# A two-layer transformer block on one core: TensorE's order in the attention loop fixed by order edges

## The chip, the core and the metric

The kernel runs on one NeuronCore of a Trainium2 chip. Five engines work side by side and meet through semaphores: TensorE (PE, matmuls, its weight loads shown as PEld), VectorE (DVE), ScalarE (ACT), GpSimd (POOL) and SyncE (SP, which here issues most of the transfers). Matmul results go to PSUM, eight banks that are read by DVE and ACT. The metric is the device time of one execution in microseconds (us), the median of the runs.

## The reference

Two layers act on 256 tokens of width 2048 and on a context of 256 tokens. Layer 0 mixes by a Fourier transform and layer 1 by attention; each ends in a projection with `w_out`. The part that matters here is layer 1:

```python
def _attend_with_sink(q, k, v, sink, mask=None):
    s = jnp.einsum('bqhgd,bkhd->bhgqk', q, k) * (ATTN_HEAD_DIM ** -0.5)
    if mask is not None:
        s = jnp.where(mask, s, NEG_INF)
    sk = jnp.broadcast_to(sink[None, :, :, None, None], s.shape[:-1] + (1,))
    p = jax.nn.softmax(jnp.concatenate([s, sk], axis=-1), axis=-1)[..., :-1]
    return jnp.einsum('bhgqk,bkhd->bqhgd', p, v)
...
    q, k, v, z = jnp.split(h @ w_in, [D_BRANCH, D_BRANCH + kvw, D_BRANCH + 2 * kvw], axis=-1)
    ...
    y = o.reshape(b, n, D_BRANCH) * jax.nn.silu(z)
x = x + gate * (y @ w_out[1])
return _rmsnorm(x, final_g)
```

There are 64 query heads of width 64 in 8 groups, each group with one key and value head. A query sees 512 keys: 256 tokens (within a window) and 256 of the context. All is float32, which the kernel reaches by splitting each operand into a high and a low half and doing three matmuls for one.

## The kernel before, in words

The program is recorded by a layer (Tile) that orders each engine's instructions by a timeline of its own, in which the order of the code is the priority, and then puts in every semaphore wait. An engine works through its list in order. `tc.issue_after(ins)` adds an edge without a wait: each instruction that the block records on the engine of `ins` stands behind `ins` in that engine's list.

The attention loop treats the 64 heads as 32 pairs. For a pair `b` there are these steps:

- **Scores** (`stage_s`, L1504): for two token blocks and two heads, 12 matmuls of 512 columns into four PSUM banks. DVE adds the mask and takes the maximum of each (L1507), ACT takes the exponentials (L1511) and that of the sink (L1513), DVE makes the factor (`sm`, L1514 and L1515). Then the weights are scaled and split: the high half on ACT (L1526), the low half on DVE (L1527, both into `f`), and SP issues a transposing transfer of each of the four `f` into `ft` (L1529). For the last pair PE transposes instead (`pe_turn`, L1397).
- **Value product** (`stage_o`, L1538): 24 small matmuls of `ft` with the values into one bank; DVE then multiplies by the gate (`emit_y`, L1487).
- **Filler units** (`emit_unit`): the projections that are still to be done, cut into 142 units: 8 for each of eight q groups, 2 for each of 32 gates z, and 14 of the first quarter of the output projection. A unit is 12 matmuls of 512 columns (q and output, L145 to L147 of `mm3`) or 24 of 256 (z). Its weights come in as `raw` (three buffers, one for two units), ACT casts the high half `wh` and DVE subtracts the low half `wl` (L66 and L67 of `split`). `wh` and `wl` share six tiles, so three units can be ready.

When a q group is done (`finish_q`), ACT copies its two PSUM banks (L1369 and L1370), POOL applies the rotary embedding (L1132 to L1138), DVE makes a scale in four tiny operations on `sq` (L1376 to L1379), and the queries are split (`fq`, L1387 on ACT, L1388 on DVE) and transposed into `qt`; the first group is transposed by PE (L1397), copied out by ACT and DVE (L1398), the others by a transfer. A group serves four pairs, and each lap of four pairs is called a head below, after its key head. The output units need `y` split into `ys` (L66, low halves on POOL). Ten units go ahead of the loop; each lap then records scores, two units, the value product of the pair before, two units, and the scheduler may shift all of these on PE against each other.

Of the kernel before, what the change touches and what calls it, by code (L numbers as in the profile page):

```python
# [17 lines left out]
P = 128  # L18
D = 2048
KT = D // P  # L20
DB = 4096
NB = DB // P
# [10 lines left out]
def tile_dit(ctx: ExitStack, tc: tile.TileContext, a: dict, out: bass.AP):  # L33
# [1106 lines left out]
    with tc.tile_pool(name="h1", reuse_waits="tile", bufs=16) as h1p:  # L1140
# [130 lines left out]
        with tc.tile_pool(name="at", reuse_waits="tile", bufs=2) as at:  # L1271
# [55 lines left out]
            def o1_step(k, os_, wh, wl):  # L1327
                while len(yh) <= min(k + 4, NB - 1) and (len(yh) < 28 or fin):
                    y_split(len(yh))
                for tb in range(2):  # L1330
                    mm3(os_[tb], yh[k][:, tb * P : (tb + 1) * P], yh[k][:, N + tb * P : N + (tb + 1) * P], wh, wl, k == 0, k == NB - 1)
            slot = [0]

            def k_turn(hp):
# [95 lines left out]
                return half_split(raws1[src], i % 2)  # L1430

            ready = {}

            def emit_unit():
                if pos[0] >= len(ulist):
                    return
                u = ulist[pos[0]]
                if pos[0] not in ready:
                    ready[pos[0]] = prep(u)
                if pos[0] + 1 < len(ulist):  # L1440
                    ready[pos[0] + 1] = prep(ulist[pos[0] + 1])
                w = ready.pop(pos[0])
                pos[0] += 1
                kind, n, i, o = u
                if kind == "o":
                    if n == 0:
                        oA.extend([psum(), psum()])
                    for j in range(2):
                        o1_step(n * 2 + j, oA, *(t[:, j * 512 : (j + 1) * 512] for t in w))
                    return  # L1450
                wh, wl = w
                if kind == "q":
                    if i == 0:
                        o += [psum(), psum()]
                    if (n, i) == (0, 4):
                        with tc.issue_after(last_cast[0]):
                            prep_kk(0)
                    for j in range(2):
                        k = i * 2 + j
                        q = slice(j * 512, (j + 1) * 512)  # L1460
                        for tb in range(2):
                            mm3(o[tb], hx1[k][:, tb * P : (tb + 1) * P], hx1[k][:, N + tb * P : N + (tb + 1) * P], wh[:, q], wl[:, q], k == 0, k == KT - 1)
                    if i == 7:
                        finish_q(n, o)
                else:
                    if i == 0:
                        o.append(psum())
                    for k in range(i * 8, i * 8 + 8):
                        q = slice((k % 8) * P, (k % 8 + 1) * P)
                        mm3(o[0][:, 0:N], wh[:, q], wl[:, q], hx1[k][:, 0:N], hx1[k][:, N : 2 * N], k == 0, k == KT - 1)  # L1470
# [20 lines left out]
            def stage_s(b):  # L1491
# [6 lines left out]
                for tb in range(2):  # L1498
                    for hh in range(2):
                        so[hh, tb] = psum()  # L1500
                    for n, (jj, kx_) in enumerate(((j, kkh), (4 + j, kkh), (j, kkl))):
                        for hh in range(2):
                            r = slice(hh * 64, hh * 64 + 64)
                            PE.matmul(so[hh, tb], qt[r, jj, tb, :], kx_[r, :], start=n == 0, stop=n == 2)  # L1504
                    for hh in range(2):
                        o = so[hh, tb]
                        V.tensor_tensor_reduce(o, o, mask[:, tb, :], sc[:, tb : tb + 1], nsink[:, 2 * b + hh : 2 * b + hh + 1], ALU.add, ALU.min, mx[:, hh, tb : tb + 1])  # L1507
# [24 lines left out]
            def stage_o(blk, pair):  # L1532
# [2 lines left out]
                steps = [(kb, c, j) for kb in range(4) for c, j in ((0, kb), (64, kb), (0, 4 + kb))]  # L1535
                for n, (kb, c, j) in enumerate(steps):
                    for hh, ft in enumerate(pair):
                        PE.matmul(oo[hh * 64 : hh * 64 + 64, :], v01[kb][:, hk, c : c + 64], ft[:, j, :, :].rearrange("p t q -> p (t q)"), start=n == 0, stop=n == len(steps) - 1)  # L1538
                obs[blk, 1] = oo
                emit_y(blk)  # L1540

# [9 lines left out]
            while defer:  # L1551
                defer.pop(0)[1]()

            def filler():
                j = slot[0]
                slot[0] += 1
                emit_unit()
                if defer and defer[0][0] + 2 < j:
                    defer.pop(0)[1]()

            pts = {}
            for b in range(33):
# [16 lines left out]
                filler()  # L1579


        with tc.tile_pool(name="fin", reuse_waits="tile", bufs=1) as fp:
# [243 lines left out]
```

## Time and profile before

| | |
|---|---|
| median of 3 runs | 1780.81 us (1779.39 to 1782.48) |
| profiled execution, time | 1778.66 us |
| its span | 1776.9 us |
| mean granted clock of PE | 0.994 |
| PE busy | 1717.7 us (97%) |
| DVE busy | 1385.8 us (78%) |
| ACT busy | 1112.8 us (63%) |
| POOL busy | 342.2 us (19%) |
| attention loop, first scores to last value product | from 1132.4 to 1636.5 us |

The profile shows one execution. Times in its rows are microseconds from the span's start. Matmuls overlap in the pipeline, so a row's duration (0.38) is longer than the distance to the next start (0.233 for 512 columns), and a busy PE is not one at its peak: the pace is read from starts. In rows of the waits, the engine behind the arrow is the one whose work came last. In rows of stretches there stand start and end, length, busy time of PE, PEld, DVE, ACT and POOL with the number of instructions, PE's granted clock, the DMA engines' busy share and GB/s. Rows of the timeline hold start, duration, engine, line, operation, tiles, shape, count and, in brackets, the idle time ahead of it and what ended it. In rows of groups stand, behind the bar, busy time and mean ns of one, then the idle time ahead of them and its releasers.

### The profile page before, as it was taken

To read this page: it belongs to the slowest core of one execution; us is meant where nothing else is said; L and a number is where in the kernel's file an instruction comes from. 1 tells how busy PE (TensorE), PEld (TensorE's weight loads), DVE (VectorE), ACT (ScalarE), POOL (GpSimd) and SP (SyncE) were. 2 spreads that over 40 slices of the span, in tenths; PEclk is the share of its full clock that TensorE was granted. 3 is DMA by queue.
4 is the path that set the end of the run, shared out by engine and by line. 5 is a ranking of instruction groups with operands and counts; after the bars stand their busy time and mean duration, and the time that the engine had idled before them with its cause. 6 is when DMAs were issued, how large, how long until landed. Compare 5 with 4: busy or idle time off the path is not lost. (4 is left out here: it accounts for less than half of the span.)

```text
span 1776.9 us, 28302 instructions
## 1 busy us (share of the span) xinstructions
PE 1717.7 (97%) x10379; PEld 1134.2 (64%) x10379; DVE 1385.8 (78%) x2334; ACT 1112.8 (63%) x2125; POOL 342.2 (19%) x485
## 2 busy tenths in 40 slices
PE   6999999999999999999999999699999999999998
PEld 4679999544444444446445646588777777877464
DVE  5779888797777796877687786878888889887755
ACT  5545556477768745465235696666677777786643
POOL 0002111212222115112311122202202220251001
PEclk9999999999999999999999999899999999999999
DMA  9998998778998969976997692588798788888643
GB/s 394 417 354 254 277 274 244 301 286 315 327 308 313 318 224 368 357 285 261 378 339 222 213 351 104 166 199 197 211 243 207 201 223 231 201 209 289 222 177 119
DMA packets 249196, 469.95 MB, mean 264 GB/s; under 512 B 171392, under 2 KB 171792, under 8 KB 222176
## 3 DMA queue, kind: packets, MB, share of 16 engines
q1 hardware_dynamic: 197568, 335.60, 57.9%
q0 software_dynamic: 47344, 125.58, 22.2%
q10 hardware_dynamic: 4144, 6.95, 1.1%
q8 instruction: 81, 1.33, 0.3%
q14 instruction: 59, 0.48, 0.1%
HBM read 419.30 MB, written 12.59 MB: 243 GB/s over the span
## 5 line engine op out<-in xcount | busy, mean ns | idle before, releaser
L67 DVE TENSOR_TENSOR wl<-raw,wh 128x1024 fp32r<-128x1024 f32 x152 | 191.5, 1270 | 101.8 <-ACT wh L66 85.8
L66 ACT CAST wh<-raw 128x1024 fp32r<-128x1024 f32 x152 | 158.1, 1046 | 81.7 <-PE ps L146 61.8
L146 PE MATMUL ps<-act,wf 128*128 128x512 f16 x512 | 194.0, 379 | 0.0
L147 PE MATMUL ps<-act,wf 128*128 128x512 f16 x512 | 191.1, 379 | 0.0
L145 PE MATMUL ps<-act,wf 128*128 128x512 f16 x512 | 189.8, 379 | 0.6 <-ACT wf L137 0.2
L145 PE MATMUL ps<-y,wf 128*128 128x512 f16 x448 | 169.8, 379 | 0.8 <-ACT wf L137 0.8
L146 PE MATMUL ps<-y,wf 128*128 128x512 f16 x448 | 169.8, 379 | 0.0
L147 PEld LDWEIGHTS <-wf 128*128 128x128 f16 x960 | 93.9, 98 | 113.1
L145 PEld LDWEIGHTS <-wf 128*128 128x128 f16 x960 | 93.7, 98 | 113.2 <-ACT wf L137 4.2
L147 PE MATMUL ps<-y,wf 128*128 128x512 f16 x448 | 164.9, 379 | 0.0
L146 PEld LDWEIGHTS <-wf 128*128 128x128 f16 x960 | 93.9, 98 | 109.1
L147 PE MATMUL ps<-h,wl 128*128 128x256 f32 x512 | 144.6, 282 | 6.3 <-DVE wl L67 6.2
L145 PE MATMUL ps<-h,wh 128*128 128x256 f32 x512 | 147.4, 288 | 0.0
L137 ACT ACTIVATE wf<-raw,nrm 128x1024 f16<-128x1024 f32 x56 | 63.5, 1146 | 131.9 <-PE ps L147 71.2
L1511 ACT ACTIVATE p<-ps,mx 128x512 f32<-128x512 f32 x128 | 87.8, 687 | 89.1 <-DVE mx L1507 84.9
L146 PE MATMUL ps<-h,wh 128*128 128x256 f32 x512 | 143.6, 280 | 0.0
L138 DVE SCALAR_TENSOR_TENSOR wf<-raw,tn,wf 128x1024 f16<-128x1024 f32 x64 | 79.8, 1282 | 42.7 <-ACT wf L137 42.6
L829 ACT ACTIVATE act<-act 128x512 f32<-128x512 f32 x178 | 109.5, 617 | 5.0 <-DMA act<-in_wo 4.5
L790 POOL DMA_DIRECT2D wa<-in_adw x64 | 34.2, 535 | 370.6 <-PE ps L147 143.1
L1527 DVE SCALAR_TENSOR_TENSOR f<-p,sm,f 128x512 f16<-128x512 f32 x128 | 104.5, 870 | 1.4 <-ACT f L1526 1.4
L145 PEld LDWEIGHTS ps<-h,wh 128*128 128x128 f32 x512 | 96.8, 189 | 10.0 <-ACT th L1474 4.2
L145 PE MATMUL ps<-wh,h 128*128 128x512 f32 x256 | 102.8, 407 | 0.0
(436 smaller groups left out, 4799.8 us busy)
## 6 DMA issues: line engine op xcount, KB each, us to landing
raw<-in_wz SPq DMA_DIRECT2D x64, 1024.0 KB, 5.3
raw<-in_awp SPq DMA_DIRECT2D x32, 1024.0 KB, 12.7
zr<-in_adw SPq DMA_DIRECT2D x64, 512.0 KB, 6.9
wa<-in_adw POOLq DMA_DIRECT2D x64, 512.0 KB, 6.6
act<-in_wo POOLq DMA_DIRECT2D x128, 256.0 KB, 7.2
raw<-in_wo SPq DMA_DIRECT2D x32, 1024.0 KB, 8.4
raw<-in_wq SPq DMA_DIRECT2D x32, 1024.0 KB, 5.4
raw<-in_wu SPq DMA_DIRECT2D x32, 1016.0 KB, 7.0
```

What stands on the lines that cost most here:

```text
L66: last_cast[0] = S.copy(h, src).ins
L67: last_sub[0] = eng.tensor_tensor(l, src, h.bitcast(F32), op=ALU.subtract).ins
L137: last_cast[0] = S.activation(w[:, 0], src, AF.Copy, scale=up).ins
L138: last_sub[0] = V.scalar_tensor_tensor(w[:, 1], src, up, w[:, 0], op0=ALU.mult, op1=ALU.subtract).ins
L145: PE.matmul(o, wh, xh, start=start, stop=False)
L146: PE.matmul(o, wh, xl, start=False, stop=False)
L147: return PE.matmul(o, wl, xh, start=False, stop=stop).ins
L790: nc.gpsimd.dma_start(wf, a["adw"][i, kh, fg][:, q])
L829: S.activation(t, t, AF.Square, accum_out=c)
L1511: S.activation(pt[hh, tb], so[hh, tb], AF.Exp, bias=mx[:, hh, tb : tb + 1], scale=-1.0, accum_out=sm[:, hh, tb : tb + 1])
L1527: f_last[:] = fa, V.scalar_tensor_tensor(f[:, 512:1024], pt[hh, tb], s1, f[:, 0:512], op0=ALU.mult, op1=ALU.subtract).ins
```

## The change

The last matmul that was recorded is kept in `pe_last[0]`: the unit's (`mm3` and `o1_step` return theirs), the scores' or the value product's. Each unit, each `stage_s` and each block of `pe_turn` and `stage_o` is recorded within `tc.issue_after(pe_last[0])`, so all of its PE instructions stand behind the last matmul of the block recorded before it. And the loop's order is another: a pair's scores, four units, the value product of the pair before, the next pair's scores. In the last lap there are three units, then the transposes and the value product, then one unit. The edges bear on PE alone; DVE, ACT, POOL and SP are ordered anew by the scheduler's timeline.

```diff
@@ o1_step
                 for tb in range(2):
-                    mm3(os_[tb], yh[k][:, tb * P : (tb + 1) * P], ...)
+                    r = mm3(os_[tb], yh[k][:, tb * P : (tb + 1) * P], ...)
+                return r
@@ emit_unit
+            pe_last = [None]
...
-                        o1_step(n * 2 + j, oA, *(t[:, j * 512 : (j + 1) * 512] for t in w))
+                        pe_last[0] = o1_step(n * 2 + j, oA, *(t[:, j * 512 : (j + 1) * 512] for t in w))
...
-                            mm3(o[tb], hx1[k][:, tb * P : (tb + 1) * P], ...)
+                            pe_last[0] = mm3(o[tb], hx1[k][:, tb * P : (tb + 1) * P], ...)
...
-                        mm3(o[0][:, 0:N], wh[:, q], wl[:, q], ...)
+                        pe_last[0] = mm3(o[0][:, 0:N], wh[:, q], wl[:, q], ...)
@@ stage_s
-                            PE.matmul(so[hh, tb], qt[r, jj, tb, :], kx_[r, :], start=n == 0, stop=n == 2)
+                            pe_last[0] = PE.matmul(so[hh, tb], qt[r, jj, tb, :], kx_[r, :], start=n == 0, stop=n == 2).ins
@@ stage_o
-                        PE.matmul(oo[hh * 64 : hh * 64 + 64, :], ...)
+                        pe_last[0] = PE.matmul(oo[hh * 64 : hh * 64 + 64, :], ...).ins
@@ the loop
-            def filler():
-                j = slot[0]
-                slot[0] += 1
-                emit_unit()
-                if defer and defer[0][0] + 2 < j:
-                    defer.pop(0)[1]()
+            def filler(n):
+                for _ in range(n):
+                    j = slot[0]
+                    slot[0] += 1
+                    with tc.issue_after(pe_last[0]):
+                        emit_unit()
+                    if defer and defer[0][0] + 2 < j:
+                        defer.pop(0)[1]()
...
                 if b < 32:
-                    pts[b] = stage_s(b)
-                filler()
-                filler()
+                    with tc.issue_after(pe_last[0]):
+                        pts[b] = stage_s(b)
+                filler(4 if b < 32 else 3)
                 if b:
                     ft, fs = pts.pop(b - 1)
-                    for (hh, tb), f in fs.items():
-                        pe_turn(ft[hh], f, tb)
-                    stage_o(b - 1, ft)
-                filler()
-                filler()
+                    with tc.issue_after(pe_last[0]):
+                        for (hh, tb), f in fs.items():
+                            pe_turn(ft[hh], f, tb)
+                        stage_o(b - 1, ft)
+                if b == 32:
+                    filler(1)
```

PE's list before, where the second pair's scores end (L1504 scores, L1538 value product, L145 to L147 units):

```order
L1504 LDWEIGHTS qt
L1504 MATMUL ps<-kkl,qt 128x512
L1538 LDWEIGHTS v
L1538 MATMUL ps<-ft,v 64x256
L145 MATMUL ps<-h_10256,wh 128x256
L146 MATMUL ps<-h_10256,wh 128x256
L147 MATMUL ps<-h_10256,wl 128x256
```

There the first matmul of pair 0's value product stands behind pair 1's scores and ahead of the unit. PE's list now, at the first matmul of that product (L1540 now):

```order
L145 MATMUL ps<-h_10659,wh 128x256
L146 MATMUL ps<-h_10659,wh 128x256
L147 MATMUL ps<-h_10659,wl 128x256
L1540 LDWEIGHTS v
L1540 MATMUL ps<-ft,v 64x256
```

It has moved behind four whole units that follow pair 1's scores. DVE's list before, from the scale of the first q group to the first scores (wl are low halves of units, ISA ps,mx a mask and its maximum):

```order
L1379 TENSOR_SCALAR sq<-sq,ksc 128x2
L67 TENSOR_TENSOR wl<-raw,wh 128x1024
L1388 SCALAR_TENSOR_TENSOR fq<-act,sq,fq 128x512 x2
L67 TENSOR_TENSOR wl<-raw,wh 128x1024 x2
L1398 COPY qt<-ps 128x8x128
L67 TENSOR_TENSOR wl<-raw,wh 128x1024 x2
L1507 ISA ps,mx<-ps,mask,nsink,sq 128x512
```

and now:

```order
L1380 TENSOR_SCALAR sq<-sq,ksc 128x2
L1389 SCALAR_TENSOR_TENSOR fq<-act,sq,fq 128x512 x2
L1399 COPY qt<-ps 128x8x128
L1509 ISA ps,mx<-ps,mask,nsink,sq 128x512
L1509 ISA mx 128x1
```

The five low halves that stood between have moved behind the first scores' masks. DVE's list before, in the lap in which a q group ends (sq is its scale, f the low halves of the softmax weights):

```order
L67 TENSOR_TENSOR wl<-raw,wh 128x1024
L1514 SCALAR_TENSOR_TENSOR sm<-sm,es 128x4
L1515 RECIPROCAL sm<-sm 128x4
L67 TENSOR_TENSOR wl<-raw,wh 128x1024
L1376 TENSOR_SCALAR sq<-sq 128x2
L1377 TENSOR_SCALAR sq<-sq 128x2
L1378 TENSOR_SCALAR sq<-sq 128x2
L1379 TENSOR_SCALAR sq<-sq,ksc 128x2
L1527 SCALAR_TENSOR_TENSOR f<-p,sm,f 128x512 x4
L67 TENSOR_TENSOR wl<-raw,wh 128x1024 x2
L1507 ISA ps,mx<-ps,mask,nsink,sq 128x512
```

and now:

```order
L1517 RECIPROCAL sm<-sm 128x4
L67 TENSOR_TENSOR wl<-raw,wh 128x1024
L1529 SCALAR_TENSOR_TENSOR f<-p,sm,f 128x512 x4
L67 TENSOR_TENSOR wl<-raw,wh 128x1024
L1377 TENSOR_SCALAR sq<-sq 128x2
L1378 TENSOR_SCALAR sq<-sq 128x2
L1379 TENSOR_SCALAR sq<-sq 128x2
L1380 TENSOR_SCALAR sq<-sq,ksc 128x2
L67 TENSOR_TENSOR wl<-raw,wh 128x1024 x2
L1477 SCALAR_TENSOR_TENSOR th<-th,ps 128x256
L1489 SCALAR_TENSOR_TENSOR act<-ps,dsc,th 128x256
L1509 ISA ps,mx<-ps,mask,nsink,sq 128x512
```

The four f have moved ahead of the scale, and the low half that stood between the masks and sm behind it.

More of the change, by code (lines that the diff above doesn't have):

```diff
@@ L1469, in emit_unit @@
                         q = slice((k % 8) * P, (k % 8 + 1) * P)
-                        mm3(o[0][:, 0:N], wh[:, q], wl[:, q], hx1[k][:, 0:N], hx1[k][:, N : 2 * N], k == 0, k == KT - 1)
+                        pe_last[0] = mm3(o[0][:, 0:N], wh[:, q], wl[:, q], hx1[k][:, 0:N], hx1[k][:, N : 2 * N], k == 0, k == KT - 1)
                     if i == 1:
@@ L1537, in stage_o @@
                     for hh, ft in enumerate(pair):
-                        PE.matmul(oo[hh * 64 : hh * 64 + 64, :], v01[kb][:, hk, c : c + 64], ft[:, j, :, :].rearrange("p t q -> p (t q)"), start=n == 0, stop=n == len(steps) - 1)
+                        pe_last[0] = PE.matmul(oo[hh * 64 : hh * 64 + 64, :], v01[kb][:, hk, c : c + 64], ft[:, j, :, :].rearrange("p t q -> p (t q)"), start=n == 0, stop=n == len(steps) - 1).ins
                 obs[blk, 1] = oo
```

4 lines of the change are left out of this document (2 added, 2 removed).

## The prediction

> **What bounds the kernel now.** I read the waits of TensorE (PE) first, over the attention loop and the stretch ahead of it. The columns are: engine, tile and line, what it waited for, microseconds in total, times, longest.
>
> ```profile
> PE ps L1538 <- ACT f L1526: 14.6, 1, 14.6
> PE ps L1538 <- DMA ft<-f: 7.1, 12, 1.0
> PE ps L147 <- DVE wl L67: 6.2, 7, 1.0
> PE ps L146 <- DVE wl L67: 2.8, 1, 2.8
> ```
>
> PE stands still once for 14.6 us and 20 times for about 1 us. Then PE's timeline at the start of the loop (start, duration, engine, line, tiles, count):
>
> ```profile
> 1126.21 1.07 PE L1397 MATMUL ps<-ident,fq 128*128 128x128 f16 x16
> ...
> 1152.88 0.39 PE L1538 MATMUL ps<-ft,v 128*64 128x256 f16 x1 [14.62 <-ACT f L1526]
> ...
> 1157.60 1.50 PE L1538 MATMUL ps<-ft,v 128*64 128x256 f16 x23
> ...
> 1176.70 0.61 PE L1504 MATMUL ps<-kkh,qt 64*128 64x512 f16 x4
> ```
>
> The long wait is one matmul of pair 0's value product, which the scheduler put on PE right behind pair 1's scores, two filler units early. The row at 1176.70 is pair 3's score. The stretches with their granted clock (second last but two):
>
> ```profile
> 1140.00:1150.00 10.00, 0.00 (x0) 0.00 (x0) 10.00 (x12) 6.55 (x15) 8.84 (x8) 0.64 0.27 52
> 1150.00:1160.00 10.00, 7.12 (x55) 6.59 (x56) 3.85 (x8) 4.83 (x9) 0.00 (x0) 0.67 0.96 145
> ```
>
> After 14.6 us of rest the clock stood at 0.64 and 0.67. Now the steady loop. Scores of one pair to scores of the next is one period:
>
> ```profile
> 1220.08 0.61 PE L1504 MATMUL ps<-kkh,qt 64*128 64x512 f16 x4
> ...
> 1225.80 0.39 PE L147 MATMUL ps<-h,wl 128*128 128x256 f32 x1 [1.00 <-DVE wl L67]
> ...
> 1229.65 1.50 PE L1538 MATMUL ps<-ft,v 128*64 128x256 f16 x23 [0.77 <-DMA ft<-f]
> ...
> 1236.94 0.60 PE L1504 MATMUL ps<-kkh,qt 64*128 64x512 f16 x4
> ...
> 1252.50 0.61 PE L1504 MATMUL ps<-kkh,qt 64*128 64x512 f16 x4
> ...
> 1266.92 0.60 PE L1504 MATMUL ps<-kkh,qt 64*128 64x512 f16 x4
> ...
> 1572.57 0.61 PE L1504 MATMUL ps<-kkh,qt 64*128 64x512 f16 x4
> ```
>
> A period without a wait takes 1266.92 - 1252.50 = 14.42. The one from 1220.08 takes 16.86, the next 15.56. From pair 3's scores (1176.70) to pair 29's (1572.57) there are 26 periods, 395.87 in all. At 14.42 they would take 374.9, so **20.9 us** are lost, about 3.5 in each of six heads (once per four pairs). PE sets the pace, and loses it where VectorE (DVE) is late.
>
> **Part 1: the first two pairs.** In the new order PE does the query transposes (L1398) after 46 unit matmuls behind d_turn, where it did 84; then scores, four units, scores, four units, pair 0's value product, scores.
>
> ```profile
> 1105.57 1.04 PE L1345 MATMUL ps<-ident,dn 128*128 128x128 f32 x8
> ...
> 1120.05 0.22 DVE L1379 TENSOR_SCALAR sq<-sq,ksc 128x2 int32<-128x2 int32 x1
> ...
> 1122.34 1.41 DVE L1388 SCALAR_TENSOR_TENSOR fq<-act,sq,fq 128x512 f16<-128x512 f32 x2
> ...
> 1121.07 1.33 ACT L1387 ACTIVATE fq<-act,sq 128x512 f16<-128x512 f32 x2
> ...
> 1126.98 1.01 ACT L1398 COPY qt<-ps 128x1024 f16<-128x1024 f16 x1 [0.17 <-PE ps L1397]
> ```
>
> A unit is 12 matmuls of 512 columns or 24 of 256, which start 0.233 or 0.117 apart, so 2.8 us. Behind d_turn (ends 1106.5) the 46 take 10.7: PE is at the transposes at 1117.3. Their input: the DVE order up to the scale (1120.05) is unchanged; then 1.33 on ACT with 1.41 on DVE half a step behind, so the first half is there at 1121.7. **PE waits 4.4 us**, a wait that before did not have. Transposes 1.1, then 0.6 more until the copy to qt (1.01) is through; the scores start at 1123.5 and end at 1124.9. Four units, scores, four units, value product, scores (11.2 + 1.4 + 11.2 + 1.5 + 1.4) end at 1151.6. The value product at 1148.7 is free: pair 0's f are written some 7 us behind its scores (4 x 0.73 of masks, 1.1, 2.74, rows below), and a transfer lands after
>
> ```profile
> ft<-f SPq DMA_TRANSPOSE x96, 3.4
> ```
>
> 3.4 us. In this first head DVE falls behind (next part's mechanism, here with the four f under the rope): I count 1.4 and 1.8 us of waits of units for their low half, so pair 3's scores start at 1151.6 + 11.2 + 3.2 + 1.5 = 1167.5. Before: 1176.70. **Gain 9.2.**
>
> The clock: from 1152.88 to 1157.60 PE did 23 of a unit's 24 matmuls in 4.7 us, where 2.7 were due, so a long rest costs 2.0 more. No row has a rest of 4.4 us; those of 1 us cost nothing (the steady loop's clock, in its row below, is 1.00), the one of 14.6 us cost 2.0. I take 1.0 (0 to 2.0): **8.2**, bounds 4 (the q chain later, both clock losses) to 10.
>
> The Trainium skill's page "TensorE: Matmul & The Clock Gate" (Part 1: The HAM clock gate) says that PE falls to half clock after an idle window of about 3.4 us and comes back after as much work. By that the new 4.4 us wait would cost an estimated 1.7 us and part 1 would give 7.5; the 0.64 above agrees with it for the long rest, and no run here shows a rest of 4 us.
>
> **Part 2: the steady loop.** The value product of a pair now comes two scores and eight units behind its own scores (28.8 us) where it came 21.7 behind. These 7 us swallow the transfer wait (0.77 and its like). What stays is DVE. Its rows in the stretch where a q group ends and POOL ropes the queries:
>
> ```profile
> 1213.50 1.29 POOL L1132 TENSOR_TENSOR act<-act,rope 128x512 f32<-128x512 f32 x1 [32.24 <-issue]
> ...
> 1219.77 2.97 POOL L1138 TENSOR_TENSOR act<-act,rt 128x512 f32<-128x512 f32 x2
> ```
>
> ```profile
> 1208.43 0.82 DVE L1507 CUSTOM_DVE_ANT_0 ps<-ps,mask,nsink 128x512 f32<-128x512 f32 x1
> ...
> 1209.16 0.82 DVE L1507 CUSTOM_DVE_ANT_0 ps<-ps,mask,nsink 128x512 f32<-128x512 f32 x1
> ...
> 1214.93 1.64 DVE L67 TENSOR_TENSOR wl<-raw,wh 128x1024 fp32r<-128x1024 f32 x1 [1.34 <-ACT wh L66]
> 1216.49 0.70 DVE L1376 TENSOR_SCALAR sq<-sq 128x2 f32<-128x2 f32 x1
> ...
> 1219.74 4.87 DVE L1527 SCALAR_TENSOR_TENSOR f<-p,sm,f 128x512 f16<-128x512 f32 x4
> 1224.54 2.35 DVE L67 TENSOR_TENSOR wl<-raw,wh 128x1024 fp32r<-128x1024 f32 x2
> ...
> 1297.47 2.74 DVE L1527 SCALAR_TENSOR_TENSOR f<-p,sm,f 128x512 f16<-128x512 f32 x4
> ```
>
> Under the rope (9.2 us) four f take 4.87 instead of 2.74, a low half 1.64 instead of 1.2, and the four tiny sq operations 3.3 (1216.49 to 1219.74). In the old order all of these stand ahead of the low halves (1224.54) for which PE waits at 1225.80. How long an exponential and a cast of ACT last:
>
> ```profile
> L66 ACT CAST wh<-raw 128x1024 fp32r<-128x1024 f32 x152 | 158.1, 1046 | 81.7 <-PE ps L146 61.8
> ...
> L1511 ACT ACTIVATE p<-ps,mx 128x512 f32<-128x512 f32 x128 | 87.8, 687 | 89.1 <-DVE mx L1507 84.9
> ```
>
> In the new order a pair is: four masks (0.73 apart, 2.9), sm, one low half, four f, three low halves. At a pair's scores three units are ready (six ws tiles), so the first low half has until 8.4 us behind the scores, the others until 14, 17 and 20. ACT casts the q psums only after its own four f, so the rope starts at 7.5 and four f escape it. I count, from the end of the scores: masks to 2.8, the last exponential with the sink's 1.1 more, ACT's cast 1.0, low half ready at 6 (due 8.4); f until 9; low half 11; sq until 14; two low halves 17; masks of the next pair from 18 (3.9 late), with the fq between; its first low half 23.4 where PE wants it at 22.7: 0.7 late. One pair on, masks end at 34.1 and the low half stands at 37.6 against 37.7, no room. I take **1.2 us per head** where now 3.5 are lost, since each hop costs some tenths that I rounded off: 6 x 1.2 = 7.2, gain **13.7**. Bounds: 0.6 per head (17.3) to 3.5 (0).
>
> The other cover is DVE's own time:
>
> ```profile
> 1176.70:1572.57 395.87, 382.45 (x2857) 313.36 (x2858) 339.03 (x560) 291.77 (x581) 71.66 (x60) 1.00 0.87 217
> ```
>
> 339.03 us of DVE in 26 periods, 13.0 a period or 52 a head, where PE needs 57.7. In the new order DVE waits for the exponentials and the cast in three pairs of four (no low half stands between masks and sm now), about 1.9 each: 52 + 5.6 = 57.7. DVE and PE then need the same.
>
> Block changes: value product and next scores now adjoin, so a period has three changes of operand instead of four.
>
> ```profile
> 1503.71 0.39 PE L147 MATMUL ps<-wh,h 128*128 128x512 f32 x1
> 1504.04 1.50 PE L1538 MATMUL ps<-ft,v 128*64 128x256 f16 x24
> 1505.47 0.50 PE L145 MATMUL ps<-wh,h 128*128 128x512 f32 x1
> 1505.80 0.40 PE L146 MATMUL ps<-wl,h 128*128 128x512 f32 x1
> ```
>
> Into and out of a value product the step is 0.33 instead of 0.233, so 0.1 a change: 28 x 0.1 = **2.8** (bounds -2.8, if scores behind a value product cost 0.2 to start, to 5.6).
>
> **Part 3: the tail.** Pair 30's and 31's scores were split and strewn among units; now all stand whole, and pair 31's transposes run as one block of 32 with the value product one matmul behind. Before, the tail lost the 2.8 us of the fourth wait row. Now ACT's 28 ys casts stand between the exponentials as before; I count 0.4, 1.1, 0.5 and 0.3 for four units' low halves and 0.5 for the copy behind the 32 transposes, 2.8: **no change** (-3 to +3).
>
> SP issues the same transfers in the same groups; a raw buffer comes free with its unit's last low half and is wanted five units later, so no weight comes late. The later stages keep their order, and PE fills its stretches there:
>
> ```profile
> 1640.00:1660.00 20.00, 20.00 (x93) 10.96 (x91) 14.80 (x15) 14.04 (x18) 3.55 (x2) 1.00 0.54 186
> ```
>
> What is won arrives at the end.
>
> **Sum.** 8.2 + 13.7 + 2.8 + 0 = 24.7 us. The profiled execution took 1778.66 (span 1776.9), so 1754.0; the median of the runs shown, 1780.81, lies 2.15 above it: **1756**. With the bounds of parts 1 and 2 (the others partly cancel) 1746 to 1768.
>
> **Rivals.**
> - The stall only changes its name (0.20): the transfer waits go, but low halves come as late as DVE allows and a head keeps losing 3.5. For it: DVE and PE need the same time, worked out above. Against: at 1225.80 PE waits behind f and sq, which now stand behind the low half due first. Then parts 1 and the changes alone: 8.2 + 2.8 = 11, 1770.
> - The start gives little (0.12): the query chain is later than read, and the clock falls. Against: its DVE order is unchanged up to 1120.05. Gain 24.7 - 6 = 19, 1762.
> - DVE becomes the bound, and the kernel slower (0.07): mechanism and place are the wait of sm behind the masks with nothing between. At 3 us in each pair a head takes 52 + 12 = 64 against 395.87 x 4 / 26 = 60.9 now: 3 x 6.5 = 20 lost against 11 won, 1790. It decides for slower from 2.6 us a pair on. Against it: the exponential of the last mask is 0.7 and the cast 1.0 long, nothing else stands between.
> - The edges do nothing (0.03): the scheduler had its order anyway. Against: PE's order differs from the first transposes on. 1781.
>
> **How the numbers follow.** The forecast has 0.58: 1756. With the first two rivals "faster" is 0.58 + 0.20 + 0.12 = 0.90, less 0.02 for small gains: 0.88; same 0.05, slower 0.07 (the bound is 0.2%, about what a measurement here can tell from no change). The range must reach to the first rival: 1746 to 1772.
>
> **What would show it.** Right: no wait of 14.6 us at L1540 and no transfer waits there; a wait of some 4.4 us at L1398 for fq; pair 3's scores near 1167.5; periods of 14.3; waits at L147 for wl of about 1 us a head. Wrong: waits for wl in every pair (DVE bound); a clock under 0.9 for more than one stretch behind 1117; pair 29's scores less than 15 us ahead of 1572.57, or waits of more than 4 us in the tail behind them.

## The result and the profile after

The changed kernel takes 1769.62 us in the median (1768.53 to 1770.66), the kernel before on the same chip 1780.1 (1779.26 to 1782.48): a ratio of **0.9939** (0.9922 to 0.9956), some 10.5 us faster. The forecast was 1756. The profiled execution took 1770.25 with a span of 1768.5, 8.4 less than the 1776.9 of before; the clock is 0.994 in both.

PE's waits over the attention loop and the stretch ahead of it, the view that the prediction began with (what waits, for what, total, times, longest):

```profile
PE ps L147 <- DVE wl L67: 7.1, 8, 1.3
PE ps L1540 <- ACT ft L1399: 6.1, 1, 6.1
PE ps L145 <- ACT wh L66: 5.4, 6, 1.7
PE ps L1398 <- ACT fq L1388: 3.7, 2, 3.4
```

The 14.6 us wait and the waits for transfers are gone. Four kinds stand in their place: for low halves as before, a new one of 6.1 us in the tail, a new one for high halves, and the foreseen one at the query transposes. PE's timeline at the places that the forecast named (L1506 are scores, L1540 value products, L1398 transposes):

```profile
1121.49 0.40 PE L1398 MATMUL ps<-ident,fq 128*128 128x128 f16 x4 [3.44 <-ACT fq L1388]
...
1123.83 1.04 PE L1506 MATMUL ps<-kkh,qt 64*128 64x512 f16 x4 [0.49 <-ACT qt L1399]
...
1169.66 0.61 PE L1506 MATMUL ps<-kkh,qt 64*128 64x512 f16 x4
...
1224.00 0.38 PE L145 MATMUL ps<-h,wh 128*128 128x256 f32 x1 [0.68 <-ACT wh L66]
...
1225.26 0.39 PE L147 MATMUL ps<-h,wl 128*128 128x256 f32 x1 [0.76 <-DVE wl L67]
...
1258.22 0.60 PE L1506 MATMUL ps<-kkh,qt 64*128 64x512 f16 x4
...
1272.50 0.61 PE L1506 MATMUL ps<-kkh,qt 64*128 64x512 f16 x4
...
1288.74 0.61 PE L1506 MATMUL ps<-kkh,qt 64*128 64x512 f16 x4
...
1557.36 0.60 PE L1506 MATMUL ps<-kkh,qt 64*128 64x512 f16 x4
...
1611.67 1.96 PE L1398 MATMUL ps<-ident,f 128*128 128x128 f16 x32
...
1619.78 0.37 PE L1540 MATMUL ps<-ft,v 128*64 128x256 f16 x1 [6.14 <-ACT ft L1399]
```

From these starts the gain divides into three. At pair 3's scores the kernel is 1176.70 - 1169.66 = **7.0** us ahead. From there to pair 29's scores it takes 387.70 where it took 395.87, **8.2** more. At pair 29 it is 15.2 ahead, at the end 8.4: the tail gives **6.8** back.

In the steady loop a period without a wait takes 14.28 (1258.22 to 1272.50; others 14.23), so 14.25 in the mean and 370.5 for 26; 17.2 us are lost, 2.9 a head. The stalled period (1272.50 to 1288.74) takes 16.24. Stretches of PE (start and end, length, busy time of PE, PEld, DVE, ACT, POOL, granted clock, DMA share, GB/s):

```profile
1120.00:1130.00 10.00, 7.59 (x43) 4.53 (x44) 6.33 (x16) 6.91 (x14) 0.00 (x0) 0.83 0.24 100
1169.66:1557.36 387.70, 376.98 (x2858) 312.91 (x2858) 343.28 (x563) 292.81 (x582) 82.04 (x60) 1.00 0.92 222
1620.00:1630.00 10.00, 10.00 (x51) 4.94 (x51) 2.65 (x6) 1.95 (x5) 0.00 (x0) 0.75 0.32 120
```

Two rests, of 3.44 and 6.14 us, leave a lower clock behind them. Next DVE, in the lap in which a q group ends:

```profile
1206.73 3.78 DVE L1529 SCALAR_TENSOR_TENSOR f<-p,sm,f 128x512 f16<-128x512 f32 x4
1210.44 1.75 DVE L67 TENSOR_TENSOR wl<-raw,wh 128x1024 fp32r<-128x1024 f32 x1
1212.11 0.70 DVE L1377 TENSOR_SCALAR sq<-sq 128x2 f32<-128x2 f32 x1
1212.85 1.20 DVE L1378 TENSOR_SCALAR sq<-sq 128x2 int32<-128x2 int32 x1
...
1215.34 3.45 DVE L67 TENSOR_TENSOR wl<-raw,wh 128x1024 fp32r<-128x1024 f32 x2
...
1219.62 0.81 DVE L1509 CUSTOM_DVE_ANT_0 ps<-ps,mask,nsink 128x512 f32<-128x512 f32 x1
```

POOL ropes from 1208.62 to 1219.9:

```profile
1208.62 1.34 POOL L1132 TENSOR_TENSOR act<-act,rope 128x512 f32<-128x512 f32 x1 [33.43 <-issue]
...
1212.75 1.26 POOL L1132 TENSOR_TENSOR act<-act,rope 128x512 f32<-128x512 f32 x1
...
1215.36 4.58 POOL L1138 TENSOR_TENSOR act<-act,rt 128x512 f32<-128x512 f32 x2
```

From the second half of the four f on, all of DVE's work up to the next masks lies under the rope and lasts longer: f 3.78 for four, low halves 1.7 each, sq from 1212.11 to 1215.34. The masks begin at 1219.62, some 5 us behind the end of their scores (started 1213.17, so done at 1214.5). ACT's exponentials and casts come behind the masks, and so PE waits at 1224.00 for a high half and at 1225.26 for a low one. POOL's two adds take 4.58 where they took 2.97 before.

A wait costs PE more than its row says. The matmul before the one at 1224.00 starts at 1223.04, and at the usual step of 0.117 the next would have started at 1223.16: 0.84 are lost where the row has 0.68, and the step behind it is 0.22 instead of 0.117. So PE's 14 waits in the steady loop, 10.7 us by their rows, cost an estimated 14.3 of the 17.2; in one head there is clock as well (below).

In the tail, ACT has the copy behind pair 31's transposes behind a cast of the next stage's weights:

```profile
1616.03 2.19 ACT L137 ACTIVATE wf<-raw,adab 128x1024 f16<-128x1024 f32 x2 [4.39 <-DMA raw<-in_wo1b]
1618.12 0.71 ACT L1312 ACTIVATE yf<-act,adab 128x512 f16<-128x512 f32 x1
1618.73 1.90 ACT L1399 COPY ft<-ps 128x1024 f16<-128x1024 f16 x2
```

The cast waits 4.39 us for a transfer, and the copy, whose data were there at 1613.6, stands behind it.

### The profile page after: what moved, and what is told of

It is laid out like the page before. It is cut to its first block, busy times and chain, and to the rows that moved or that the text cites. A ratio compares the mean times of both kernels' runs of the same rounds, so it can differ in the third digit from the quotient of the medians.

```text
span 1768.5 us, 28328 instructions
## 1 busy us (share of the span) xinstructions
PE 1714.7 (97%) x10379; PEld 1133.7 (64%) x10379; DVE 1390.4 (79%) x2334; ACT 1111.0 (63%) x2125; POOL 352.8 (20%) x485
## 5 line engine op out<-in xcount | busy, mean ns | idle before, releaser
L67 DVE TENSOR_TENSOR wl<-raw,wh 128x1024 fp32r<-128x1024 f32 x152 | 200.1, 1337 | 43.7 <-ACT wh L66 35.2
L147 PE MATMUL ps<-act,wf 128*128 128x512 f16 x512 | 191.1, 379 | 0.0
L145 PE MATMUL ps<-act,wf 128*128 128x512 f16 x512 | 189.8, 379 | 0.6 <-ACT wf L137 0.2
L145 PE MATMUL ps<-y,wf 128*128 128x512 f16 x448 | 169.8, 379 | 0.8 <-ACT wf L137 0.8
L147 PEld LDWEIGHTS <-wf 128*128 128x128 f16 x960 | 93.9, 98 | 113.3
L145 PEld LDWEIGHTS <-wf 128*128 128x128 f16 x960 | 93.7, 98 | 113.3 <-ACT wf L137 4.2
L147 PE MATMUL ps<-y,wf 128*128 128x512 f16 x448 | 164.9, 379 | 0.0
L147 PE MATMUL ps<-h,wl 128*128 128x256 f32 x512 | 144.4, 282 | 7.1 <-DVE wl L67 7.1
L145 PE MATMUL ps<-h,wh 128*128 128x256 f32 x512 | 145.9, 285 | 5.4 <-ACT wh L66 5.4
L790 POOL DMA_DIRECT2D wa<-in_adw x64 | 34.1, 532 | 370.5 <-PE ps L147 140.0
L145 PEld LDWEIGHTS ps<-h,wh 128*128 128x128 f32 x512 | 96.8, 189 | 13.7 <-ACT wh L66 7.0
L146 PE MATMUL ps<-wl,h 128*128 128x512 f32 x256 | 101.9, 398 | 0.8 <-DVE wl L67 0.8
L147 PEld LDWEIGHTS ps<-h,wl 128*128 128x128 f32 x512 | 96.8, 189 | 8.7 <-DVE wl L67 8.7
```

Source lines behind the costliest of these rows:

```text
L67: last_sub[0] = eng.tensor_tensor(l, src, h.bitcast(F32), op=ALU.subtract).ins
L145: PE.matmul(o, wh, xh, start=start, stop=False)
L146: PE.matmul(o, wh, xl, start=False, stop=False)
L147: return PE.matmul(o, wl, xh, start=False, stop=stop).ins
L790: nc.gpsimd.dma_start(wf, a["adw"][i, kh, fg][:, q])
```

## The experiments

All times are medians, and ratios are against the kernel before, run on the same chip (1780.92 to 1781.43). The letters of the theories are those of each expectation. In the first ones A says that the tail's wait is ACT's order and no necessity, B that the low halves are late because POOL's rope stretches DVE's work, C that a queue waits for the rope's result.

**The tail alone.** Pair 31's transposes go two units earlier, so that its value product has two units behind them.

```diff
-                filler(4 if b < 32 else 3)
+                filler(4 if b < 32 else 2)
...
+                    if b == 32:
+                        with tc.issue_after(pe_last[0]):
+                            for (hh, tb), f in fs.items():
+                                pe_turn(ft[hh], f, tb)
+                        filler(2)
                     with tc.issue_after(pe_last[0]):
-                        for (hh, tb), f in fs.items():
-                            pe_turn(ft[hh], f, tb)
                         stage_o(b - 1, ft)
-                if b == 32:
-                    filler(1)
```

> The changed kernel (1769.6 us median) with one edit in the last lap: two units, pair 31's transposes, two units, then its value product (the changed kernel has three units, transposes, value product at once, one unit). Theory A, the copy from PSUM stands in ACT's list behind a weight cast that waits for a late transfer, and PE, with nothing between transposes and value product, waits 6.1 us for it and then runs at a low clock (the 22 matmuls behind the first one took 7.6 us where 4.8 are due): two units (5.6 us) between them hide the copy, the wait falls under 1 us, the clock stays at 1.00, 7 to 9 us are won: 1761 to 1763. Rival, the weights of the output projection are late for PE itself: the wait moves to the first units of the projection, at most 2 us are won: 1768 to 1770.

1760.72 us, ratio 0.9884 (0.9869 to 0.9898). PE's transposes and first value product there:

```profile
1610.22 1.96 PE L1398 MATMUL ps<-ident,f 128*128 128x128 f16 x32
...
1617.75 0.30 PE L1540 MATMUL ps<-ft,v 128*64 128x256 f16 x1
```

No wait there, and the clock is 1.00 from 1610 to 1630; the 8.9 us that are won are the 6.14 of the wait and some 2.6 of clock (in the changed kernel, 12 matmuls of the next stage behind the wait started 0.43 apart where 0.215 is usual). From pair 29's scores to the end it takes 201.8 us, the changed kernel 211.1, the kernel before 204.3. The steady loop takes 386.45, close to the changed kernel's 387.70. So A holds.

**Without the rope.** The rope of q groups 1 to 7 is left out.

```diff
-                        roped(t, t0, tb, actp, "act", GP)
+                        t = t0
```

> The changed kernel without the rotary embedding of q groups 1 to 7 on POOL (the queries go on unrotated, so this part of the computation is left out; ACT's copies, the scale, fq and all other work stay, and all lists of PE, DVE and ACT are the same). In the changed kernel a head loses 2 to 4.5 us (mean 2.9) in the pair behind the end of a q group. Theory B, contention: the POOL work slows the DVE operations beside it (two low halves take 3.5 to 4.6 us instead of 2.35, the four sq 3.3 instead of 0.6), so masks and the next low half come late. Without it a head loses under 1 us: 12 to 16 us won, 1754 to 1758. Theory C, the queue: ACT's fq stands ahead of the exponentials and waits for the rope's result. Without it the same gain. Theory D, DVE as a whole is the bound, whatever POOL does: 3 us or less won, 1766 to 1769.

**The rope for nothing.** POOL does the rope, but its result is not used, so nothing waits for it.

```diff
                         roped(t, t0, tb, actp, "act", GP)
+                        t = t0
```

> The same, but POOL still does the rope's operations on the same data at the same time; only its result is not used (the queries go on unrotated, so the rotation is left out of the result). It tells contention from dependence. Theory B (contention): a head still loses 2 us or more, as in the changed kernel, 0 to 3 us won, 1766 to 1770. Theory C (fq waits on ACT ahead of the exponentials): the loss goes as without the rope, 12 to 16 us won, 1754 to 1758.

Without the rope 1748.59, ratio 0.9816 (0.9801 to 0.983), with the idle rope 1768.1, ratio 0.9923 (0.9907 to 0.994). In the trace without the rope, pair 3's to pair 29's scores take 369.72, 14.22 a period: nothing is lost at all. With the idle rope they take 386.44, as in the changed kernel, though ACT's split of the queries no longer waits for POOL (the changed kernel has 29.9 us of such waits there, up to 3.87 each). C falls. DVE's groups in this stretch (behind the bar: busy time, mean ns), in the changed kernel:

```profile
L67 DVE TENSOR_TENSOR wl<-raw,wh 128x1024 fp32r<-128x1024 f32 x106 | 138.8, 1334 | 14.1 <-ACT wh L66 14.0
L1509 DVE CUSTOM_DVE_ANT_0 ps<-ps,mask,nsink 128x512 f32<-128x512 f32 x104 | 78.8, 814 | 0.0
L1529 DVE SCALAR_TENSOR_TENSOR f<-p,sm,f 128x512 f16<-128x512 f32 x106 | 78.8, 804 | 0.0
...
L1378 DVE TENSOR_SCALAR sq<-sq 128x2 int32<-128x2 int32 x6 | 7.2, 1199 | 0.2
```

and without the rope:

```profile
L67 DVE TENSOR_TENSOR wl<-raw,wh 128x1024 fp32r<-128x1024 f32 x106 | 128.4, 1224 | 29.8 <-ACT wh L66 29.1 <-PE ps L146 0.6
L1509 DVE CUSTOM_DVE_ANT_0 ps<-ps,mask,nsink 128x512 f32<-128x512 f32 x104 | 78.8, 816 | 0.0
L1529 DVE SCALAR_TENSOR_TENSOR f<-p,sm,f 128x512 f16<-128x512 f32 x104 | 71.1, 746 | 0.0
```

Low halves and f last longer on the mean with the rope beside them, an operation on two columns takes 1.2 us, and the masks, which read PSUM, last the same. DVE is busy 309.70 instead of 343.28 us. B holds as to the cause, and the gain (21 us, of which 18 in the steady loop and 3.6 ahead of pair 3's scores) was larger than expected.

**Edges alone, lists alone.** First the edges with the old order of the loop (two units, value product, two units), then the new order without edges.

```diff
-                filler(4 if b < 32 else 3)
+                filler(2)
...
-                if b == 32:
-                    filler(1)
+                filler(2)
```

> The order edges alone, with the old loop order (scores, two units, value product of the pair before, two units); in the last lap two units, transposes, value product, two units. Against before (1780.1) it differs by the edges, against the changed kernel by the loop order. Theory: the edges alone take away the 14.6 us wait of pair 0's value product (pair 3's scores near 1169 to 1171 as in the changed kernel, 6 to 8 us won), the transfer waits of the value product (about 1 us in each q group's end, since its slack is 21.7 us again) and four block changes a period (14.42) stay, so 26 periods from pair 3's to pair 29's scores take 394 to 396; the tail has the same wait for the copy behind the transposes, 6 to 9 us lost: 1777 to 1782. Rival, the loop order is what changes DVE's list and brings the rope's contention onto the low halves: then 26 periods take less than in the changed kernel (387.7) and the kernel is near 1770.

```diff
-                    with tc.issue_after(pe_last[0]):
+                    with nullcontext():
                         emit_unit()
...
-                    with tc.issue_after(pe_last[0]):
+                    with nullcontext():
                         pts[b] = stage_s(b)
...
-                    with tc.issue_after(pe_last[0]):
+                    with nullcontext():
                         for (hh, tb), f in fs.items():
```

> The changed lists of work (scores, four units, value product of the preceding pair) without the order edges; nothing is left out of the computation. Theory A (the lists alone set TensorE's order, the edges only confirm it): 1768 to 1771, pair 3's scores near 1169.7, a period of 14.25. Theory B (the scheduler again pulls matmuls together as it did before: a value product directly behind scores, a long wait in the first pair): 1777 to 1783, with one wait of over 10 us near 1150 and waits for the transfer of f.

The edges alone give 1776.58, just under what was expected, ratio 0.997 (0.9961 to 0.9979); the lists alone 1779.26, ratio 0.9986 (0.9969 to 1.0002). With the edges alone the start gains 8.4 (pair 3's scores at 1168.35), the steady loop takes 397.14, and the transfer waits stay (7.1 ahead at pair 29's scores, 1.4 at the end):

```profile
PE ps L1540 <- DMA ft<-f: 8.3, 15, 0.9
```

With the lists alone PE's list is pulled apart again, as B said, though the long wait is smaller than B had it (8.9 us for f in pair 0's value product, where over 10 was expected) and of the transfer waits only one of 0.3 came back. In the steady loop, which takes 397.94, the product is cut up:

```profile
1258.67 0.30 PE L1540 MATMUL ps<-ft,v 128*64 128x256 f16 x2
1259.56 0.41 PE L1540 MATMUL ps<-ft,v 128*64 128x256 f16 x4
1262.43 1.17 PE L1540 MATMUL ps<-ft,v 128*64 128x256 f16 x18
```

Each cut is a change of operand, and such a period takes 14.86 where one with a whole product takes 14.28. This kernel's runs lie further apart than the others' (1772.72 to 1786.60), and the profiled one is 4.6 under the median. So the change is both parts together: neither alone gives much.

**The rope on VectorE.** For all groups DVE ropes the queries straight from PSUM; ACT's copy goes.

```diff
-                        t0 = act()
-                        S.copy(t0, oq[tb])
...
-                        roped(t, t0, tb, actp, "act", GP)
+                        roped(t, oq[tb], tb, actp, "act")
```

> The changed kernel, with the rope of the query groups 1 to 7 on VectorE, straight from PSUM (as group 0 has it), in place of ACT's copy and GpSimd's rope; nothing is left out. From the rows: on VectorE a tile's rope is 0.68 + 2 x 0.41 + 0.69 = 2.19, two tiles 4.4 us a head; with the rope gone from GpSimd VectorE's busy time in the steady loop fell from 343.3 to 309.7, 5.2 us a head. Theory B (what costs is VectorE's time in that pair, whoever takes it): 0.8 us a head less of lateness, some 5 us in all: 1763 to 1768. Theory D (the loss hangs on GpSimd working beside VectorE, not on VectorE's sum): most of the 18 us that leaving the rope out gave come back, 1750 to 1757. Theory E (VectorE has no room where the queries come, 4.4 us in one piece is worse than stretched small work): over 1771.

1751.11, ratio 0.9827 (0.9811 to 0.9844): D. The steady loop takes 370.41 (1168.30 to 1538.71):

```profile
1168.30:1538.71 370.41, 370.41 (x2858) 310.58 (x2856) 329.20 (x609) 285.46 (x568) 19.16 (x12) 1.00 0.95 232
```

The same work, on the engine that was thought to be short of time, loses nothing: DVE is busy 329.20 with the rope on it and was 343.28 with the rope beside it.

**Twelve units ahead of the loop.** Two units are taken from the last lap and put ahead of the loop; the last lap is mended as above.

```diff
-            first = 10
+            first = 12
...
-                filler(4 if b < 32 else 3)
+                filler(4 if b < 32 else 0)
...
+                    if b == 32:
+                        with tc.issue_after(pe_last[0]):
+                            for (hh, tb), f in fs.items():
+                                pe_turn(ft[hh], f, tb)
+                        filler(2)
```

> Twelve units ahead of the loop instead of ten, and in the last lap the transposes of pair 31 at once, then two units, then its value product; nothing is left out. Reference: the kernel with the tail alone mended, 1760.7. The 3.4 us rest of TensorE ahead of the query transposes should fall away, and the low clock behind it. Theory A (the rest costs itself and some 1.3 us of clock): 1755.5 to 1757.5, no stretch under 0.95 at 1120. Rival (VectorE's lateness in the first head takes the time back, as pair 2 and 3 already wait for their low halves): 1759 to 1762, with longer waits for wl between 1150 and 1185.

**With the rope on VectorE as well:**

```diff
-            first = 10
+            first = 12
...
-                        roped(t, t0, tb, actp, "act", GP)
+                        roped(t, oq[tb], tb, actp, "act")
```

> The twelve units ahead, the last lap's order and the rope on VectorE together; nothing is left out. If the three add up: the time of the kernel with twelve units ahead, less what the rope on VectorE gives beside the changed kernel. Theory B: 1750 to 1753. Theory D: 1738 to 1745. Theory E: over 1757.

1735.71, ratio 0.9742 (0.9727 to 0.9757), and 1733.88, ratio 0.9731 (0.9712 to 0.9749). The first is 20 us faster than either theory had it, and the second lies below all three of its theories. The rope on VectorE adds nothing that can be told: 1.8 us between the medians, with intervals that overlap. The steady loop with twelve units, POOL still roping:

```profile
1120.00:1130.00 10.00, 9.10 (x56) 6.23 (x55) 7.78 (x16) 8.69 (x16) 0.00 (x0) 1.00 0.53 202
1166.85:1538.60 371.75, 371.75 (x2858) 310.10 (x2857) 323.39 (x560) 293.48 (x587) 73.99 (x63) 1.00 0.99 231
```

PE waits nowhere in it. This did not fit B as it stood: the rope was there, and cost nothing. A lap (here one pair's turn) has four units, and a head has eight q units and eight z units, which are four laps, so every group ends at the same place in its lap. With ten units ahead of the loop that is the lap's second unit, with twelve its last. POOL's adds and DVE there, at a group's end (POOL ropes from 1194.15 to 1203.6):

```profile
1201.06 2.55 POOL L1138 TENSOR_TENSOR act<-act,rt 128x512 f32<-128x512 f32 x2
```

```profile
1195.57 1.59 DVE L67 TENSOR_TENSOR wl<-raw,wh 128x1024 fp32r<-128x1024 f32 x1 [0.63 <-ACT wh L66]
...
1198.43 0.81 DVE L1509 CUSTOM_DVE_ANT_0 ps<-ps,mask,nsink 128x512 f32<-128x512 f32 x1
...
1202.30 1.34 DVE L1380 TENSOR_SCALAR sq<-sq,ksc 128x2 int32<-128x2 int32 x1
...
1204.47 1.22 DVE L67 TENSOR_TENSOR wl<-raw,wh 128x1024 fp32r<-128x1024 f32 x1
1205.61 2.73 DVE L1529 SCALAR_TENSOR_TENSOR f<-p,sm,f 128x512 f16<-128x512 f32 x4
```

The rope now lies over the masks, which are not stretched (0.81), and over sq and one low half; f and the other low halves up to the next masks come behind it, at their usual length. Over the steady loop the low halves take 127.9 us (138.8 in the changed kernel) and f 71.8 (78.8), while the operations on sq take 20.9 (20.0): sq is as slow as it was, and that costs PE nothing here. From this came theory P: the place of a group's end in the lap decides. Its rival R: the greater lead is what helps.

**Six units in the first lap**, ten ahead, so that the place moves and the start stays (the last lap as with twelve):

```diff
-                filler(4 if b < 32 else 3)
+                filler(6 if b == 0 else 4 if b < 32 else 0)
```

> Ten units ahead of the loop as in the changed kernel, but six units instead of four behind the first pair's scores, and the last lap as in the kernel with twelve units; nothing is left out. TensorE's rest and the low clock at the query transposes stay; from pair 1 on a query group ends with the last unit of a lap, as with twelve units, instead of with the second. Theory P (the place of a group's end in the lap decides: the same rope then lies under the masks and costs TensorE nothing): pair 3's to pair 29's scores 370 to 373, time 1738 to 1743. Theory R (the two units more ahead of the first scores are what helps, by the rest that falls away or the greater lead of the loads): 384 to 388 as before, 1756 to 1762.

**Fourteen units ahead**, so that the lead grows and the place is the old one (the rest as with twelve):

```diff
-            first = 10
+            first = 14
```

> Fourteen units ahead of the loop instead of twelve, so that none is left for the last lap behind pair 31's transposes; nothing is left out. A query group ends with the second unit of a lap again, as with ten. Theory P (its place in the lap decides): pair 3's to pair 29's scores 382 to 388, six periods of 16 to 17; with some 6 us of wait at the last value product 1754 to 1760. Theory R (the lead ahead of the loop helps): 370 to 373 and 1741 to 1745.

**The kernel before with twelve units**, nothing else changed:

```diff
-            first = 10
+            first = 12
```

> The kernel before, with its own order, and twelve units ahead of the loop instead of ten; nothing is left out. Here too a query group then ends with the last unit of a lap. Theory P: most of the 20.9 us that its steady loop loses go, the 14.6 us wait of the first value product stays: pair 3's to pair 29's scores 376 to 382, time 1762 to 1770. Rival (in the old order the low halves stand behind f whatever the place of the rope, so the waits stay): over 390 and 1776 to 1783.

1741.81, ratio 0.978 (0.9765 to 0.9794); 1775.43, ratio 0.9967 (0.9954 to 0.9979); 1754.12, ratio 0.9848 (0.9834 to 0.9863). Pair 3's to pair 29's scores, in this order:

```profile
1172.17:1544.13 371.96, 371.88 (x2858) 310.02 (x2857) 323.56 (x559) 292.74 (x586) 73.95 (x62) 1.00 0.99 230
```

```profile
1179.70:1577.33 397.63, 383.71 (x2858) 321.38 (x2858) 337.54 (x554) 294.94 (x592) 92.06 (x73) 0.97 0.88 214
```

```profile
1180.37:1556.88 376.51, 376.33 (x2857) 311.11 (x2856) 326.73 (x559) 295.23 (x588) 71.10 (x64) 1.00 0.92 227
```

The loop goes as P says in all three, and R falls: with fourteen the units are furthest ahead of the pairs and the loss is back. There it is even larger than P had it, 27 us or 4.5 a head, and the time 15 us over what P expected: behind two rests, of 1.56 and 0.76, that end 1.26 apart, the clock falls in each head (mean 0.97 over the stretch; 0.67 here):

```profile
1220.00:1224.00 4.00, 3.24 (x15) 3.04 (x16) 4.00 (x6) 4.00 (x7) 0.00 (x0) 0.67 0.64 152
```

Why the first rest is 1.56 in every head here, where the changed kernel has 0.25 to 0.68 in four of its six, stays open.

The kernel before loses 376.5 - 374.9 = 1.6 us in its steady loop with twelve units where it lost 20.9, in its old order with its one long wait (12.0 us) still there. At 1754.12 it is 15.5 us faster than the changed kernel with ten, and some 8 faster than expected. Of the 23.8 us between the spans of the two profiles 19.4 lie in the steady loop, some 2 ahead of it and 2.5 in the tail, which lost a wait of 2.8 (the two units, 5.7 us, counted where they now stand); between the medians there are 27.3.

## Why the prediction was wrong

**What bounds the kernel** was read right: PE sets the pace and loses it where DVE is late. What makes DVE late was only half read. The stretch under the rope was quoted (four f 4.87 instead of 2.74, a low half 1.64), but taken as a load that a better order would move out of the way. In the prediction's terms the forecast was 8.2 + 13.7 + 2.8 + 0; measured are 7.0 + 3.7 + 4.4 - 6.8 = 8.3.

**Part 1** came out at 7.0 of 8.2. The wait at the transposes is 3.44 where 4.4 was counted, the copy 0.49 for 0.6, the waits for low halves 1.2 and 1.3 for 1.4 and 1.8, and pair 3's scores start at 1169.66, for 1167.5 and the 1.0 us of clock that was added. Of the 1.2 that are missing 0.5 were lost ahead of it all: d_turn starts at 1106.11 where it started at 1105.57. The clock was the part sized too small: it fell to 0.83 in the stretch behind the rest, and the scores took 2.7 us instead of 1.4. The kernels with six units in the first lap and with twelve ahead have done the same 24 units at pair 3's scores and are 1172.17 - 1166.85 = 5.3 us apart, so the rest of 3.44 cost some 1.9 more. The sentence on the Trainium skill's page "TensorE: Matmul & The Clock Gate" (Part 1: The HAM clock gate), by which the new rest would cost an estimated 1.7 us of clock, was nearer than the 1.0 taken, and a rest of that length has now been seen.

**Part 2 is the step that failed**: "I take 1.2 us per head where now 3.5 are lost". It is 2.9, so part 2 gave 20.9 - 17.2 = 3.7 instead of 13.7. What the count had for low halves (5) and sq (3) under the rope is near the trace (5.2 and 3.2). Wrong was "four f escape it", which the count's own times deny (rope from 7.5, f until 9): POOL starts at 1208.62 and f run from 1206.73 to 1210.5, 3.78 where 2.74 is usual, so all that stands behind them on DVE is later. The next masks come 5.1 late where 3.9 were counted. The low half behind them ends at 1225.2, and by its usual pace PE would have used it at 1223.4: 1.9 late where 0.7 was counted. The count also had only the low half. ACT's cast stands behind exponentials that wait for the masks, and PE waits for its high half first: 1.4 us of waits in the head at 1224 (its period takes 16.31, 2.1 over 14.25), 2.4 in the one at 1344. In one head these rests cost clock as well:

```profile
1222.00:1226.00 4.00, 2.56 (x20) 2.15 (x19) 3.65 (x8) 4.00 (x12) 0.00 (x0) 1.00 0.57 106
1340.00:1344.00 4.00, 2.35 (x19) 2.00 (x17) 3.98 (x10) 3.86 (x10) 0.00 (x0) 1.00 0.27 71
1344.00:1348.00 4.00, 3.25 (x17) 3.19 (x17) 3.68 (x7) 4.00 (x10) 0.00 (x0) 0.64 0.94 212
...
1524.00:1528.00 4.00, 3.52 (x36) 3.39 (x38) 3.68 (x8) 4.00 (x8) 0.00 (x0) 1.00 0.92 242
```

The period with the head at 1344 takes 18.80. The new order did take f and sq from ahead of the low half that is due first, but the other low halves lie under the rope. The transfer waits went, as said. And "DVE and PE then need the same" was no bound: with twelve units DVE is busy 323 of 372 us and PE never waits. The reasoning left out what decided most in these runs, where in the lap the group ends.

**Block changes** gave more than said: a period without a wait went from 14.42 to 14.25, 4.4 us in 26, where 2.8 was forecast. (14.42 was the shorter of two: the next period before, 1266.92 to 1281.40, takes 14.48, so the gain here is rather larger and the 20.9 rather smaller.)

**Part 3 failed too**: "0.5 for the copy behind the 32 transposes" was 6.1, with some 2.6 of clock behind it, and so the tail lost 6.8 instead of nothing. "so no weight comes late" holds for the units' weights; the next stage's came late, and ACT's list has their cast ahead of the copy.

Of the rivals, "the stall only changes its name" gave 1770 and comes nearest in time, with a loss of 2.9 a head near its 3.5; but its sum had 5.4 less from the steady loop and no loss in the tail, so part of the agreement is chance. "DVE becomes the bound" is answered by the steady loop that lost nothing with all of the rope on DVE.

## What to carry to other kernels

When a fixed cycle of fillers feeds a periodic loop, ask on which filler of a lap each helper's work falls: here, shifting the cycle by two fillers gave 27 us to the old order and 25 to the new one with its tail mended (some 5 of them the rest at the start), where the new order by itself gave 10.5. A count of an engine's time has to use the stretched durations for everything that will lie beside the other engine, and to follow how that engine's work moves along. And before a block is closed up with edges, look on every engine at what stands ahead of its first consumer, in the tail above all.

## What the runs showed of the hardware

GpSimd's tensor work lengthened VectorE's operations that read two tiles of SBUF, and not its masks, which read PSUM and one tile: low halves from 1.22 to 1.7, four f from 2.74 to 3.78 (before: 4.87), the masks 0.81 in both, also with the rope beside them (twelve units). It goes both ways: two adds of GpSimd took 4.58 beside low halves and 2.55 beside two operations on sq. The Trainium skill's "GPSIMD Engine Reference" (1. Specifications) says that GpSimd shares its SBUF interfaces with VectorE and contends with operations on two SBUF inputs or in a two-port mode; the trace agrees as to f and low halves, which have two such inputs.

The operations on sq (128x2) have one input, so this doesn't cover them unless they run in a two-port mode, which no row shows. Without the rope they take 0.16 to 0.22, beside it 0.65 to 1.20, and what they wait for can be read: the one at 1212.85 lasts until 1214.05, GpSimd's operation from 1212.75 until 1214.01. All 24 of them in the changed kernel's steady loop end within some 0.05 us of the end of a GpSimd operation (where one row holds two of these, it is halved); with twelve units 18 of 24 do, and the first of each four, at 0.31, does not. They are not slowed in proportion to their size; they last until GpSimd's current operation is over.

What all this cost was decided by place: 17 us in one phase, about 1 in another.

The clock also fell where PE never rested for long: rests of 1.65 and 0.75 us that end 1.26 apart were followed by 0.64 in the stretch at 1344, while rests of 0.68 and 0.76 left it at 1.00. Rests of 1.72 and 0.76 near 1524 left it at 1.00 too (last row of the fence above), so their length alone does not decide. In the kernel with the tail alone mended, whose edit lies in the last lap, the longer rest and the fall came in another head (1.70 and 0.75 near 1229, clock 0.68 from 1228 to 1232), so the program does not fix the head either. What decides was not tried.
